# Five matmuls of a two-layer decoder trunk issued in two pieces each

## The chip, the cores and the metric

The kernel runs on one core of a Trainium2 chip. The metric is the device time of one execution in microseconds (us), the median of several runs.

## The reference

The input is x (256 tokens by 1024 features, float32) and a conditioning vector c. Two layers follow each other; each has a token mixer and then a gated feed-forward, and each of these four sub-layers is `x <- x + gate(c) * f(rmsnorm(x) * (1 + scale(c)) + shift(c))`:

```
mod = silu(c) @ w_ada[i] + b_ada[i]            # shift, scale, gate for mixer and feed-forward
layer 0 mixer: 8 heads of 128, causal attention inside one block of 256, QK RMS-norm
layer 1 mixer: b, c, u = split(h @ w_in);  y = (b * conv3(c * u)) @ w_out
feed-forward:  g, u = split(h @ w_gate_up);  y = (silu(g) * u) @ w_down      # width 2816
```

## The kernel before

All activations stay on the chip, features on the 128 partitions and the 256 tokens along the free dimension. Weights stream from HBM in tiles of 128 partitions by 8 x 256 float32 (1 MB), which SyncE's DMA queue loads into five `wf` buffers (`load`, L88). A float32 product is made of three products on TensorE: ScalarE rounds a weight tile to fp32r (`wh`, L98), VectorE takes the rest (`wl`, L99), both into three rotating buffers, and the activations are held in the same two parts. `mm3` (L246 to L250) issues the three matmuls of one 128x128 weight block by 256 token columns:

```
    def mm3(ps, lhs, rhs, first, last):
        (ah, al), (bh, bl) = lhs, rhs
        nc.tensor.matmul(ps, ah, bh, ...)   # L248
        nc.tensor.matmul(ps, ah, bl, ...)   # L249
        nc.tensor.matmul(ps, al, bh, ...)   # L250
```

The first operand is the stationary one; in the trace each matmul has a weight load of its own, even where the second matmul of a triple uses the same block as the first. `feat_gemm` runs over eight k (128 input features each) and two o (halves of 256 output features) and calls `mm3`: 48 matmuls for one weight tile.

The program in order: an opening with modulation sums and the first q/k products; attention and its output projection (`op_o`); the first feed-forward; the convolution; its output projection (`op_co`); the second feed-forward. A feed-forward (`ffn`, L426) has eleven steps j. Step 0 is `raw_gemm`: products of 258 columns (`raw_f`, `raw_m`) that run while the norm is still being made, ended by `settle`, two matmuls of one bf16 column (L396). Steps 1 to 10 are two `feat_gemm` each, gate (`pg`) and up (`pu`), 96 matmuls. Then `out_proj` makes `op_d`, 528 matmuls. The convolution has four steps with `pc`, `pu` and `pb`, of which step 0 takes `pc` and `pu` from `raw_gemm`.

VectorE also makes the modulation columns of the later sub-layers (`ada_piece`, `prod`, L109) between the weight tiles. A tile scheduler sets the order on each engine; weight tiles are asked for two ahead (`get`, AHEAD = 2). TensorE's instructions stand in program order.

Of the kernel before, what the change touches and what calls it, by code (L numbers as in the profile page):

```python
# [16 lines left out]
S = 256  # L17
D = 1024
KD = D // P
# [14 lines left out]
def trunk_kernel(ctx: ExitStack, tc: tile.TileContext, x_t, cols_in, scale_in, shift_in, ada_in, qk_rows, kv_in, o_in,  # L34
                 in_in, out_in, gu_in, down_in, out_f):
    nc = tc.nc
# [7 lines left out]
    def ps_gemm(name):  # L44
        return psum.tile([P, 2, CW], F32, tag="gemm", name=name, bufs=4)
# [104 lines left out]
    def new_pair(tag, name, nk):  # L150
        return tuple(pair_rows(room(tag + p, nk * S, name + p, F32R)) for p in "hl")
# [3 lines left out]
    hs = new_pair("h", "m0", KD)  # L155
# [11 lines left out]
    def conv_col(j, k):  # L167
        return v_cols[:, 32 + j * KD + k:][:, :1]
# [62 lines left out]
    def produce(upto):  # L231
        while pos[0] < len(chunks) and pos[0] <= upto:
            ch = chunks[pos[0]]
            if ch[0] == "a":
                ada_piece(*ch[1:])
            else:
                ready[ch[1]] = prep(ch[2], ch[3], "_".join(map(str, ch[1])), ch[1] in first_two)
            pos[0] += 1

    def get(key):  # L240
        n = place[key]
        produce(order[min(n + AHEAD, len(order) - 1)])
        return ready.pop(key)


    def mm3(ps, lhs, rhs, first, last):  # L246
        (ah, al), (bh, bl) = lhs, rhs
        nc.tensor.matmul(ps, ah, bh, start=first, stop=False, skip_group_check=True)  # L248
        nc.tensor.matmul(ps, ah, bl, start=False, stop=False, skip_group_check=True)  # L249
        nc.tensor.matmul(ps, al, bh, start=False, stop=last, skip_group_check=True)  # L250

    def feat_gemm(parts, xs, nk):
        xh, xl = xs
        for k in range(nk):
            for ps, (wh, wl) in parts:
                for o in range(2):
                    cs = slice(o * P, (o + 1) * P)
                    mm3(ps[:, o], (wh[:, k, cs], wl[:, k, cs]), (xh[:, k], xl[:, k]),
                        k == 0 and o == 0, k == nk - 1)

    def tok_gemm(parts, xs, nk, between={}):
        xh, xl = xs
        for k in range(nk):
            for fn, *args in between.get(k, ()):
                fn(*args)
            for ps, (wh, wl) in parts:
                for t in range(2):
                    ts = slice(t * P, (t + 1) * P)
                    mm3(ps[:, t], (xh[:, k, ts], xl[:, k, ts]), (wh[:, k], wl[:, k]),
                        k == 0 and t == 0, k == nk - 1)  # L270
# [117 lines left out]
    def split(dst, k, src, name, psum_src=False):  # L388
        nc.scalar.activation(dst[0][:, k], src, AF.Copy)
        nc.vector.tensor_sub(dst[1][:, k], src, dst[0][:, k].bitcast(F32))  # L390
# [7 lines left out]
    def raw_gemm(keys, norm, name):  # L398


        raw = norm.raw
        pss = [[psum.tile([P, S + 2], F32, tag=tag, name=f"raw_{name}_{i}{o}", bufs=n) for o in range(2)]
               for i, (tag, n) in enumerate((("gemm", 4), ("alt", 2)))]
        ws = [get(k) for k in keys]
        for k in range(KD):
            if k == 2:
                norm.rstd()
            if k == 4:
                rows = norm.rows()
                with tc.high_priority(400):  # L410
                    hs = modulated(norm.l, norm.sh, norm.scl, rows, name)
            for ps, (wh, wl) in zip(pss, ws):
                for o in range(2):
                    cs = slice(o * P, (o + 1) * P)
                    mm3(ps[o], (wh[:, k, cs], wl[:, k, cs]), (raw[0][:, k], raw[1][:, k]), k == 0, k == KD - 1)
        settle(name)
        res = []
        for i, tag in enumerate("sa"):
            y = tmp.tile([P, 2, S], F32, tag=tag, name=f"rawy_{name}_{i}")
            b = tmp.tile([P, 2], F32, tag="rawb", name=f"rawb_{name}_{i}")  # L420
            for o in range(2):
                nc.vector.tensor_copy(b[:, o:o + 1], pss[i][o][:, S:S + 1])
                nc.vector.tensor_mul(y[:, o], pss[i][o][:, :S], rows)
            res.append((y, b))
        return res[0], res[1], hs

    def ffn(l, norm, av, done):
        for j in range(KF // 2):
            if j == 0:
                (s, bs), (a, ba), hs = raw_gemm([("g", l, j), ("u", l, j)], norm, f"f{l}")  # L430
                for o in range(2):
                    nc.scalar.activation(s[:, o], s[:, o], AF.Silu, bias=bs[:, o:o + 1])
                    nc.vector.scalar_tensor_tensor(a[:, o], a[:, o], ba[:, o:o + 1], s[:, o], op0=ALU.add,
                                                   op1=ALU.mult)
            else:
                pg, pu = ps_gemm(f"pg_{l}_{j}"), ps_gemm(f"pu_{l}_{j}")
                feat_gemm([(pg, get(("g", l, j)))], hs, KD)
                feat_gemm([(pu, get(("u", l, j)))], hs, KD)
                s = tmp.tile([P, 2, S], F32, tag="s", name=f"s_{l}_{j}")
                nc.scalar.activation(s, pg, AF.Silu)  # L440
                a = tmp.tile([P, 2, S], F32, tag="a", name=f"a_{l}_{j}")
                nc.vector.tensor_mul(a, s, pu)
            split(av, slice(2 * j, 2 * j + 2), a, f"{l}_{j}")
        out_proj([[(("d", l, j, i), n) for i, n in enumerate((8, 8, 6))] for j in range(4)], av, l, G_F, done)
# [15 lines left out]
    def mod_columns(y, name):  # L460

        ps = ps_misc(f"mod_c_{name}")
        n = y.shape[1] // P
        for i in range(n):
            nc.tensor.matmul(ps[:, i:i + 1], y[:, i * P:(i + 1) * P], firsts, start=True, stop=True)
        return ps[:, :n]
# [71 lines left out]
    with tc.manual_schedule(engines={mybir.EngineType.PE, mybir.EngineType.DVE, mybir.EngineType.Activation}):  # L538
# [13 lines left out]
        for k in range(KD):  # L552
            nc.tensor.matmul(c_ps[k // 4][:, k % 4 * P:][:, :P], sc[:, k:k + 1].to_broadcast([P, P]), ident, start=True,
                             stop=True)
# [18 lines left out]
        ps = mod_columns(y, "sc0")  # L573
# [181 lines left out]
    zv, zraw = wide_pair("zv")  # L755
    n1 = Norm("n1", 1, SH_M, SC_M, zraw)
    ffn(0, n0, av, n1.take)


# [3 lines left out]
    for j in range(4):  # L763
        up = ups[j % 2]
        if j == 0:
            (cg, bc), (cu, bu), hs = raw_gemm([("cg", j), ("cu", j)], n1, "m1")
            for o in range(2):
                nc.scalar.activation(cg[:, o], cg[:, o], AF.Identity, bias=bc[:, o:o + 1])
                nc.vector.scalar_tensor_tensor(up[:, o, 2:], cu[:, o], bu[:, o:o + 1], cg[:, o], op0=ALU.add,
                                               op1=ALU.mult)  # L770
        else:
            pc, pu = ps_gemm(f"pc_{j}"), ps_gemm(f"pu_{j}")
            feat_gemm([(pc, get(("cg", j)))], hs, KD)
            feat_gemm([(pu, get(("cu", j)))], hs, KD)
            cg = tmp.tile([P, 2, S], F32, tag="s", name=f"cg_{j}")
            nc.scalar.activation(cg, pc, AF.Copy)
            with tc.high_priority(400):
                nc.vector.tensor_mul(up[:, :, 2:], cg, pu)
        pb = (ps_alt2 if j else ps_gemm)(f"pb_{j}")
        feat_gemm([(pb, get(("cb", j)))], hs, KD)  # L780
        y = tmp.tile([P, 2, S], F32, tag="a", name=f"y_{j}")
        with tc.high_priority(400):
            for o in range(2):
                k = 2 * j + o
                nc.scalar.activation(y[:, o], up[:, o, 0:S], AF.Copy, scale=conv_col(0, k))
            for i in (1, 2):
                for o in range(2):
                    nc.vector.scalar_tensor_tensor(y[:, o], up[:, o, i:i + S], conv_col(i, 2 * j + o), y[:, o],
                                                   op0=ALU.mult, op1=ALU.add)
        z = tmp.tile([P, 2, S], F32, tag="s", name=f"z_{j}")  # L790
        with tc.high_priority(400):
            nc.vector.tensor_mul(z, y, pb)
            split(zv, slice(2 * j, 2 * j + 2), z, f"z{j}")
# [6 lines left out]
    def store(k):  # L800
        if k >= KD - 2:
            nc.sync.dma_start(out_f[:, k], xT[:, k])
        elif k % 2:
            nc.sync.dma_start(out_f[:, k - 1:k + 1], xT[:, k - 1:k + 1])

    ffn(1, n2, av, store)


# [58 lines left out]
```

## Time and profile before

| what | value |
|---|---|
| runs | 597.25, 598.31, 599.61 us; median 598.31 |
| profiled execution | 597.81 us, span of its instructions 596.0 us |
| TensorE, weight loads | busy 587.8 and 579.0 us of the span |
| VectorE, ScalarE | busy 454.5 and 314.1 us |
| granted TensorE clock | 1.000 |
| DMA | 156 MB, 262 GB/s over the span |

The profile has one row for every matmul and one for every weight load (PEld). A row's start is measured; a matmul's end is modelled, and a row of 0.28 us overlaps the two that follow, so a busy TensorE can still be running at more than one pace. What shows the pace is the distance between starts.

### The profile page before, as it was taken

What the parts mean: (1) busy time and instruction counts of PE and PEld (TensorE: products, weight loads), DVE (VectorE), ACT (ScalarE), POOL (GpSimd) and SP (SyncE); (2) the same over time, 40 slices, a digit from 0 to 9 for tenths busy, and PEclk for the clock granted to TensorE, in tenths of its full rate; (3) what the DMA queues carried; (4) which work ended last, traced back from release to release, by engine and by line L of the source; (5) the groups of instructions that cost most, each with busy time, mean ns of one, the idle gap of its engine ahead of it and who ended that gap; (6) DMA issues with size and microseconds to landing.
All of it is one profiled execution on the core that took longest, in us unless ns stands there. A gap on an engine that the chain in (4) does not pass through costs nothing.

```text
span 596.0 us, 12024 instructions
## 1 busy us (share of the span) xinstructions
PE 587.8 (99%) x5036; PEld 579.0 (97%) x5036; DVE 454.5 (76%) x719; ACT 314.1 (53%) x526; POOL 1.1 (0%) x8
## 2 busy tenths in 40 slices
PE   7999999999999999999999999999999999999997
PEld 6899999999999999999999999999999999999997
DVE  4789898898988879877877998659987566564440
ACT  6457799596544544534444754437844554443330
POOL 0000000000000000000000000000000000000000
PEclk9999999999999999999999999999999999999999
DMA  8999988945897899777987477544486574655400
GB/s 323 392 373 411 361 332 300 369 162 180 329 388 296 303 358 356 268 279 276 330 317 292 148 293 278 207 142 184 170 323 249 206 283 164 252 186 190 165 19 18
DMA packets 25109, 156.04 MB, mean 262 GB/s; under 512 B 2784, under 2 KB 3168, under 8 KB 8928
## 3 DMA queue, kind: packets, MB, share of 16 engines
q1 hardware_dynamic: 25056, 155.28, 69.9%
q8 instruction: 39, 0.64, 0.4%
q14 instruction: 14, 0.11, 0.1%
HBM read 154.22 MB, written 1.05 MB: 261 GB/s over the span
## 4 chain that ended last, share of the span: by engine, by line
PE 89%; DVE 4%; DMA 3%; ACT 2%; issue 1%; SPq 0%; DVEq 0%; ACTq 0%
PE pu L250 7%; PE pu L249 7%; PE pu L248 7%; PE op_d L249 7%; PE op_d L248 7%; PE op_d L250 7%; PE pg L249 6%; PE pg L248 6%; PE pg L250 6%; PE op_o L248 1%; PE raw_f L248 1%; PE raw_f L249 1%; PE op_o L250 1%; PE op_co L250 1%; PE raw_f L250 1%; DMA wa<-in_ada_dram 1%
## 5 line engine op out<-in xcount | busy, mean ns | idle before, releaser
L109 DVE SCALAR_TENSOR_TENSOR prod<-wa,c_all 128x1024 f32<-128x1024 f32 x80 | 97.6, 1220 | 13.9 <-DMA wa<-in_ada_dram 13.0
L98 ACT ACTIVATE wh_d<-wf_d 128x1024 fp32r<-128x1024 f32 (+1 forms) x48 | 45.3, 981 | 67.2 <-issue 46.5
L99 DVE TENSOR_TENSOR wl_d<-wf_d,wh_d 128x1024 fp32r<-128x1024 f32 (+1 forms) x48 | 52.9, 1132 | 26.4 <-ACT wh_d L98 26.4
L98 ACT ACTIVATE wh_g<-wf_g 128x1024 fp32r<-128x1024 f32 x44 | 45.7, 1051 | 47.0 <-issue 47.0
L98 ACT ACTIVATE wh_u<-wf_u 128x1024 fp32r<-128x1024 f32 x44 | 44.5, 1051 | 48.4 <-issue 48.0
L99 DVE TENSOR_TENSOR wl_u<-wf_u,wh_u 128x1024 fp32r<-128x1024 f32 x44 | 52.2, 1219 | 16.7 <-ACT wh_u L98 16.5
L99 DVE TENSOR_TENSOR wl_g<-wf_g,wh_g 128x1024 fp32r<-128x1024 f32 x44 | 53.3, 1219 | 2.5 <-ACT wh_g L98 2.4
L249 PE MATMUL op_d<-a0l,wh_d 128*128 128x256 f32 x176 | 49.3, 280 | 0.0
L248 PE MATMUL op_d<-a0h,wh_d 128*128 128x256 f32 x176 | 49.1, 279 | 0.0
L250 PE MATMUL op_d<-a0h,wl_d 128*128 128x256 f32 x176 | 49.1, 279 | 0.0
L248 PE MATMUL op_d<-a1h,wh_d 128*128 128x256 f32 x176 | 48.6, 276 | 0.0
L249 PE MATMUL op_d<-a1l,wh_d 128*128 128x256 f32 x176 | 48.6, 276 | 0.0
L250 PE MATMUL op_d<-a1h,wl_d 128*128 128x256 f32 x176 | 48.6, 276 | 0.0
L249 PE MATMUL pg<-f0l,wh_g 128*128 128x256 f32 x160 | 44.8, 280 | 0.0
L249 PE MATMUL pu<-f0l,wh_u 128*128 128x256 f32 x160 | 44.8, 280 | 0.0
L248 PE MATMUL pg<-f0h,wh_g 128*128 128x256 f32 x160 | 44.7, 280 | 0.0
L250 PE MATMUL pg<-f0h,wl_g 128*128 128x256 f32 x160 | 44.6, 279 | 0.0
L248 PE MATMUL pu<-f0h,wh_u 128*128 128x256 f32 x160 | 44.6, 279 | 0.0
L250 PE MATMUL pu<-f0h,wl_u 128*128 128x256 f32 x160 | 44.6, 279 | 0.0
L248 PE MATMUL pg<-f1h,wh_g 128*128 128x256 f32 x160 | 44.2, 277 | 0.0
L249 PE MATMUL pg<-f1l,wh_g 128*128 128x256 f32 x160 | 44.2, 276 | 0.0
L250 PE MATMUL pg<-f1h,wl_g 128*128 128x256 f32 x160 | 44.2, 276 | 0.0
(296 smaller groups left out, 2024.8 us busy)
## 6 DMA issues: line engine op xcount, KB each, us to landing
wa<-in_ada_dram SPq DMA_DIRECT2D x40, 1024.0 KB, 5.3
wf_g<-in_gate_up_dram SPq DMA_DIRECT2D x22, 1024.0 KB, 4.9
wf_u<-in_gate_up_dram SPq DMA_DIRECT2D x22, 1024.0 KB, 4.9
wf_d<-in_down_dram SPq DMA_DIRECT2D x16, 1024.0 KB, 5.3
wf_d<-in_down_dram SPq DMA_DIRECT2D x8, 768.0 KB, 5.4
wa_sc<-in_scale_dram SPq DMA_DIRECT2D x8, 512.0 KB, 6.7
wa_sh<-in_shift_dram SPq DMA_DIRECT2D x8, 512.0 KB, 7.6
wf_qk<-in_qk_rows_dram SPq DMA_DIRECT2D x8, 512.0 KB, 6.5
```

The costliest lines, as they stand in the source:

```text
L98: nc.scalar.activation(wh[:, a:b], wf[:, a:b], AF.Copy)
L99: nc.vector.tensor_sub(wl[:, a:b], wf[:, a:b], wh[:, a:b].bitcast(F32))
L109: nc.vector.scalar_tensor_tensor(t, w, 1.0, c_all, op0=ALU.mult, op1=ALU.mult, accum_out=dst)
L248: nc.tensor.matmul(ps, ah, bh, start=first, stop=False, skip_group_check=True)
L249: nc.tensor.matmul(ps, ah, bl, start=False, stop=False, skip_group_check=True)
L250: nc.tensor.matmul(ps, al, bh, start=False, stop=last, skip_group_check=True)
```

## The change

`mm3` takes an argument `cut`. Where it is not zero, the third product is issued as two matmuls, one of the first `cut` columns and one of the rest, each with its own load of the same weight block. `feat_gemm` takes a list of cuts and spends one at each odd k with o = 1. The first feed-forward's `pg` of step 1 gets the cuts 128, 64, 192 and 96 (k = 1, 3, 5, 7); the convolution's `pc` of step 1 gets one cut of 128 (k = 1). Nothing else in the arithmetic changes, and the sums land in the same places.

```diff
-    def mm3(ps, lhs, rhs, first, last):
+    def mm3(ps, lhs, rhs, first, last, cut=0):
...
-        nc.tensor.matmul(ps, al, bh, start=False, stop=last, skip_group_check=True)
+        for a, b in ((0, cut), (cut, S)) if cut else ((0, None),):
+            nc.tensor.matmul(ps[:, a:b], al, bh[:, a:b], start=False, stop=last, skip_group_check=True)
 
-    def feat_gemm(parts, xs, nk):
+    def feat_gemm(parts, xs, nk, cuts=()):
+        cuts = list(cuts)
...
-                        k == 0 and o == 0, k == nk - 1)
+                        k == 0 and o == 0, k == nk - 1, cuts.pop(0) if o and k % 2 and cuts else 0)
...
-                feat_gemm([(pg, get(("g", l, j)))], hs, KD)
+                feat_gemm([(pg, get(("g", l, j)))], hs, KD, (128, 64, 192, 96) if (l, j) == (0, 1) else ())
...
-            feat_gemm([(pc, get(("cg", j)))], hs, KD)
+            feat_gemm([(pc, get(("cg", j)))], hs, KD, (128,) if j == 1 else ())
```

On TensorE, in the first feed-forward's step 1 (`pg_1`; `f0h`, `f0l` are the two parts of the activations, `wh_g_1`, `wl_g_1` those of the weights), the changed program has, from the first cut to the first matmul of `pu_1`:

```order
L248 MATMUL pg_1_1995<-f0h,wh_g_1_1816 128x256
L249 MATMUL pg_1_1995<-f0l,wh_g_1_1816 128x256
L252 MATMUL pg_1_1995<-f0h,wl_g_1_1817 128x128 x2
...
L252 MATMUL pg_1_1995<-f0h,wl_g_1_1817 128x64
L252 MATMUL pg_1_1995<-f0h,wl_g_1_1817 128x192
...
L252 MATMUL pg_1_1995<-f0h,wl_g_1_1817 128x96
L252 MATMUL pg_1_1995<-f0h,wl_g_1_1817 128x160
L248 MATMUL pu_1_1996<-f0h,wh_u_1_1824 128x256
```

Before, each pair was one row of 128x256 (at L250; the line is L252 now). The first pair is the twelfth matmul of `pg_1`, the others follow twelve matmuls apart; the third, of 192 and 64 columns, is left out above. With the one pair in the convolution's `pc_1` there are five, and no other row of TensorE moves up to the end of the program.

VectorE's rows are ordered a little differently, since the scheduler sees TensorE's added instructions. Behind the second half of `wl_u_2` stood before:

```order
L109 SCALAR_TENSOR_TENSOR prod_5_0_0_2119,mod<-wa_5_0_2117,c_all 128x1024
L442 TENSOR_TENSOR a_1_2111<-s_1_2109,pu_1_1996 128x512
L109 SCALAR_TENSOR_TENSOR prod_5_0_1_2121,mod<-wa_5_0_2117,c_all 128x1024
L99 TENSOR_TENSOR wl_g_3_2126<-wf_g_3_2123,wh_g_3_2125 128x1024
L390 TENSOR_TENSOR a0l<-a_1_2111,a0h 128x512
L99 TENSOR_TENSOR wl_g_3_2126<-wf_g_3_2123,wh_g_3_2125 128x1024
```

and stands now:

```order
L109 SCALAR_TENSOR_TENSOR prod_5_0_0_2123,mod<-wa_5_0_2121,c_all 128x1024
L109 SCALAR_TENSOR_TENSOR prod_5_0_1_2125,mod<-wa_5_0_2121,c_all 128x1024
L446 TENSOR_TENSOR a_1_2115<-s_1_2113,pu_1_1996 128x512
L99 TENSOR_TENSOR wl_g_3_2130<-wf_g_3_2127,wh_g_3_2129 128x1024 x2
L394 TENSOR_TENSOR a0l<-a_1_2115,a0h 128x512
```

One modulation sum (`prod`) and one half of `wl_g_3` stand ahead of work that they stood behind. Some twenty rows of VectorE and a few of ScalarE change places by one or two in this way, in the steps up to 5 of the first feed-forward and in the convolution. SyncE's order of DMAs is the same.

## Rows read from the trace of the kernel before

**Rows 1.** The profile page: the span, the busy time of the engines (with its share of the span and the instructions), and the shares of the chain that ended last.
```profile
span 596.0 us, 12024 instructions
...
PE 587.8 (99%) x5036; PEld 579.0 (97%) x5036; DVE 454.5 (76%) x719; ACT 314.1 (53%) x526; POOL 1.1 (0%) x8
...
PE 89%; DVE 4%; DMA 3%; ACT 2%; issue 1%; SPq 0%; DVEq 0%; ACTq 0%
```

**Rows 2.** Busy time by stretch: the first feed-forward behind its step 0, the convolution with its projection, the second feed-forward behind its step 0. Columns: the stretch, its length, busy us of each engine (x instructions), the granted clock, the DMA engines' mean busy share, GB/s.
```profile
143.60:318.40 174.80, 174.80 (x1486) 174.80 (x1485) 148.21 (x210) 81.15 (x104) 0.00 (x0) 1.00 0.82 306
331.20:411.00 79.80, 79.49 (x672) 79.09 (x672) 64.08 (x104) 44.38 (x67) 0.00 (x0) 1.00 0.55 203
424.00:590.00 166.00, 166.00 (x1466) 166.00 (x1466) 99.90 (x119) 73.15 (x88) 0.00 (x0) 1.00 0.52 189
```

**Rows 3.** The tile `op_d` of the first feed-forward, every third matmul (L249): duration in ns (least, median, most), first and last start in us.
```profile
L249 PE MATMUL op_d<-a0l,wh_d x176: 280/280/280, 256.4 to 318.2; 128*128 128x256 f32 x176
```

**Rows 4.** The same of the second feed-forward, from 547.4 us on.
```profile
L249 PE MATMUL op_d<-a1l,wh_d x133: 276/276/276, 547.4 to 592.3; 128*128 128x256 f32 x133
```

**Rows 5.** Timeline of matmuls and weight loads inside the two feed-forwards. Columns: start us, us, engine, line, operation, out<-in, size.
```profile
200.06 0.19 PEld L249 LDWEIGHTS pg<-f0l,wh_g 128*128 128x128 f32 x1
200.18 0.28 PE L249 MATMUL pg<-f0l,wh_g 128*128 128x256 f32 x1
...
500.02 0.19 PEld L249 LDWEIGHTS pg<-f1l,wh_g 128*128 128x128 f32 x1
500.13 0.28 PE L249 MATMUL pg<-f1l,wh_g 128*128 128x256 f32 x1
```

**Rows 6.** Timeline of TensorE in the opening, where the q products (weights stationary) are followed without a break by the k products (activations stationary).
```profile
27.43 0.28 PE L249 MATMUL pq<-m0l,wh_qk 128*128 128x256 f32 x1
...
28.02 0.28 PE L248 MATMUL pk<-wh_qk,m0h 128*128 128x256 f32 x1
...
28.37 0.28 PE L248 MATMUL pk<-wh_qk,m0h 128*128 128x256 f32 x1
...
28.71 0.28 PE L248 MATMUL pk<-wh_qk,m0h 128*128 128x256 f32 x1
```

**Rows 7.** Timeline of TensorE in the attention: four transposes of 128 columns inside the k products.
```profile
59.55 0.60 PE L654 MATMUL q_cols<-ident,q_y 128*128 128x128 f32 x4
59.90 0.37 PE L248 MATMUL pk<-wh_k,m0h 128*128 128x256 f32 x1
...
60.23 0.28 PE L250 MATMUL pk<-wh_k,m0l 128*128 128x256 f32 x1
...
60.68 0.28 PE L248 MATMUL pk<-wh_k,m0h 128*128 128x256 f32 x1
```

**Rows 8.** Timeline of TensorE in the projection `op_o`, around a short pause at 119 us.
```profile
118.62 0.28 PE L249 MATMUL op_o<-ovl,wh_o 128*128 128x256 f32 x1
...
118.86 0.28 PE L249 MATMUL op_o<-ovl,wh_o 128*128 128x256 f32 x1
...
119.13 0.38 PE L248 MATMUL op_o<-ovh,wh_o 128*128 128x256 f32 x1
119.35 0.28 PE L249 MATMUL op_o<-ovl,wh_o 128*128 128x256 f32 x1
...
119.69 0.28 PE L249 MATMUL op_o<-ovl,wh_o 128*128 128x256 f32 x1
```

**Rows 9.** The same, around a short pause at 127 us.
```profile
126.49 0.28 PE L250 MATMUL op_o<-ovh,wl_o 128*128 128x256 f32 x1
...
126.94 0.28 PE L248 MATMUL op_o<-ovh,wh_o 128*128 128x256 f32 x1
...
127.37 0.28 PE L248 MATMUL op_o<-ovh,wh_o 128*128 128x256 f32 x1
...
127.73 0.28 PE L248 MATMUL op_o<-ovh,wh_o 128*128 128x256 f32 x1
```

**Rows 10.** Timeline of TensorE at the first feed-forward's `settle`, the two matmuls of one column, and behind it.
```profile
143.02 0.20 PE L396 MATMUL settle_f<-one_b 128*128 128x1 bf16 x2
143.09 0.36 PE L248 MATMUL pg<-f0h,wh_g 128*128 128x256 f32 x1
143.29 0.28 PE L249 MATMUL pg<-f0l,wh_g 128*128 128x256 f32 x1
```

**Rows 11.** Timeline of TensorE in the convolution's step 1, at the third matmul of `pu`.
```profile
342.84 0.28 PE L249 MATMUL pu<-m1l,wh_cu 128*128 128x256 f32 x1
343.43 0.39 PE L250 MATMUL pu<-m1h,wl_cu 128*128 128x256 f32 x1 [0.31 <-DVE wl_cu L99]
343.66 0.28 PE L248 MATMUL pu<-m1h,wh_cu 128*128 128x256 f32 x1
...
344.01 0.28 PE L248 MATMUL pu<-m1h,wh_cu 128*128 128x256 f32 x1
```

**Rows 12.** Timeline of VectorE: the second half of `wl_cu` for that `pu`.
```profile
342.16 1.22 DVE L99 TENSOR_TENSOR wl_cu<-wf_cu,wh_cu 128x1024 fp32r<-128x1024 f32 x1
```

**Rows 13.** Timeline of VectorE and of TensorE: the second half of `wl_g` of the first feed-forward's step 2, and the matmul that first reads it.
```profile
150.15 1.22 DVE L99 TENSOR_TENSOR wl_g<-wf_g,wh_g 128x1024 fp32r<-128x1024 f32 x1
...
154.71 0.28 PE L250 MATMUL pg<-f0h,wl_g 128*128 128x256 f32 x1
```

## The prediction

> **What bounds the kernel now.** I read the page first: TensorE is busy 99% of the span, its weight loads 97%, and TensorE holds 89% of the chain that ended last [rows 1]. So the time is made on TensorE, and the question is what sets the distance between two matmuls there. I then took busy times by stretch. Three long stretches have the same kind of matmul (128x128 weights, 256 columns), all at granted clock 1.00, which is the 2.4 GHz level, and all with TensorE busy throughout. Yet the first feed-forward shows 1486 matmuls in 174.8 us, 117.6 ns each, the convolution 672 in 79.8 us, 118.8 ns with its pauses, and the second feed-forward 1466 in 166.0 us, 113.2 ns [rows 2].
>
> The tile view says the same without edges. In the first feed-forward's `op_d` every third matmul starts 61.8 us / 175 = 353.1 ns after the one before, 117.7 ns a matmul; in the second 44.9 us / 132 = 340.2 ns, 113.4 ns [rows 3, 4]. The durations are constant to the nanosecond (280 and 276 ns), so these are two steady paces, not a mean of fast and slow pieces. I call them the slow and the fast pace; they differ by 4.4 ns, 3.8%.
>
> Where the 4.4 ns sit is seen beside the loads. The load for a matmul starts with the matmul before it, and the matmul starts 0.12 us after its load began in the slow stretch, 0.11 us in the fast one [rows 5]. So each matmul waits for its own weights, and the chain load, matmul, next load is a little longer at the slow pace. VectorE is not the reason: the same program text in the second feed-forward is only better supplied (VectorE 60% busy there, 85% in the first), but both paces also stand within `op_o`, a few microseconds apart with the same tiles [rows 8, 9].
>
> What changes the pace is the last thing to read. In the opening the q products run at (28.02 − 27.43)/5 = 118 ns; where operands change places and k products follow, without any idle time, the pace is (28.71 − 28.37)/3 = 113 ns [rows 6]. In `op_o` a pause of some 0.15 us turned 120 ns into 113 ns, and another turned 113 ns back into 120 ns [rows 8, 9]. Four transposes of 128 columns left fast products fast: (60.68 − 60.23)/4 = 113 ns [rows 7]. So a pace holds until something uneven comes, and is then settled anew. In the first feed-forward nothing uneven comes for the 1484 matmuls behind its start.
>
> **The change part by part.**
>
> *The first feed-forward's four cuts.* Each replaces one matmul by two, with one more weight load. No row has a 256-column product cut in two, so I bound the price of the extra matmul. From below: the two one-column matmuls of `settle` pass in 0.07 us together, 0.035 us each [rows 10]. From above: a start behind a pause is followed by the next only 0.23 us later [rows 11]. The nearest rows are the matmuls that wait for their own load, 0.11 us [rows 5], since the piece has a full 128x128 load too; the transposes of 128 columns take 0.35/4 = 0.09 us each to the next start [rows 7]. I take 0.113 us: four cost 0.45 us (ends 0.14 and 0.92).
>
> *What the cuts do to the pace.* This is the large term. I read the rows so: the load and the columns of the matmul before it run side by side [rows 5], and at the slow pace they hold each other up by 4.4 ns each time. A piece of 64 to 192 columns ends its stream early, so the load behind it should not be held up, and the chain starts again from another place. I expect that one of four unlike pieces brings the fast pace, and that the fast pace, where the load alone sets the time, is not lost to a shorter stream (the transposes did not end it [rows 7]). Behind the first cut stand 10 × 96 − 12 + 528 = 1476 matmuls, up to the end of `op_d`: 1476 × 4.4 ns = 6.5 us. If only the fourth cut does it, 36 fewer, 0.16 us less. At the worst the term is nothing, or the pace stays slow.
>
> Two pages speak against this term. The Trainium skill, in "TensorE: Matmul & The Clock Gate", section "Wait — 56ns, not 53.3ns?", gives back-to-back matmuls one distance for a column count, columns ÷ 2.4 GHz plus about 2.5 ns; that is an estimate of 109 ns at 256 columns, and the cuts would add some 0.01 us and save nothing. This trace has two distances for one shape, both longer, so here the measurement decides. The same page, section "Step-by-step: what each phase is for", says that loading the next weights takes no read bandwidth from the running matmul; by that the length of a piece could not matter, which is the first rival below.
>
> *VectorE, ScalarE and the queues.* The supply must now come 3.8% sooner. VectorE is busy 148.2 of 174.8 us [rows 2]; the fast stretch would have 168.3 us, so 88%, and DMA goes from 0.82 to 0.85. The tightest weights are those of step 2: their second half is ready at 151.4 us and first read at 154.7 us [rows 13], 3.3 us of cover against 0.43 us a step. The scheduler's swap puts one modulation sum in front of a half weight tile, 1.2 us of the cover. I take nothing; were the cover gone, the first wait would be at `pg_3`, some 1 us.
>
> *The convolution's cut.* It stands in `pc_1`, ahead of a wait that no cut removes: the third matmul of `pu_1` waits for VectorE's second half of `wl_cu`, which ends at 343.4 us, and starts 0.59 us behind its forerunner instead of 0.12 [rows 11, 12]. The extra 0.113 us lies in those 0.47 us, and so does whatever 36 faster matmuls would gain (0.16 us). Behind the wait the pace is settled anew; before, it came out slow, (344.01 − 343.66)/3 = 117 ns [rows 11]. I take the slow pace again: 0 us.
>
> *The sum.* −6.5 + 0.45 = −6.0 us. The profiled execution took 597.81 us, 1.8 us around its span; it becomes 591.8. The median of the runs lies 0.5 us higher, so I forecast 592.3 us.
>
> **The rivals.**
>
> *The pace stays slow.* The cuts cost their slots and nothing else: 598.3 + 0.45 = 598.8 us. For it: four pairs are few, and `settle`, also a short disturbance, left the first feed-forward slow. Against it: the paces did change at lesser events [rows 6].
>
> *The convolution goes fast too.* Behind its wait stand 46 + 48 + 288 + 192 = 574 matmuls; × 4.4 ns = 2.5 us, 589.8 us. The wait's new start decides, and it moves by tenths of a microsecond with what stands before.
>
> *The second feed-forward falls to the slow pace.* It is fast today behind the same `settle` that left the first slow. Its pace is decided at about 424 us, behind products of 258 columns; what comes in there is changed only if the convolution or its wait is. Price 1488 × 4.4 = 6.5 us. With the gain in the first it ends at 592.3 + 6.5 = 598.8, no change; without that gain at 598.8 + 6.5 = **605.3 us, slower**. Its sign is the pace of `pg` just behind 424 us.
>
> *Supply too late.* The first feed-forward goes fast but waits for weights: 592.3 plus 1 to 3 us.
>
> That the change does not do what it says I rule out: TensorE's order has the five pairs and nothing else.
>
> **How the numbers follow.** A measurement of this kernel can tell 0.5%, 3.0 us, from no change. Chances: first feed-forward fast alone 0.30 (592.3); convolution too 0.26 (589.8); pace stays slow 0.22 (598.8); gain in the first and loss in the second feed-forward 0.12 (about 598.8, or 596.3 with the convolution); loss alone 0.07 (605.3); late supply 0.03. Faster is the first two and half of the last: 0.58. Slower is the loss alone and an unforeseen wait: 0.08. The rest, 0.34, is within 0.5%. The forecast's own range is 591.2 to 593.4 us, the scatter of the runs. The range for 8 in 10 must reach from the convolution's case, 589.8 less 1.0 for scatter, to the slow pace with its dearer cuts (598.3 + 0.92, rounded up): 588.8 to 599.4 us. It leaves the loss alone outside.
>
> **What would show it.** Right: `op_d` of the first feed-forward at 340 ns for three, the change of pace within the 48 matmuls of `pg_1`, the stretch from there to the end of `op_d` near 168 us, the wait at `pu_1` still there, and 353 ns for three behind it. The extra slots are wrong if the second piece of a pair starts more than 0.2 us behind the first. The whole is wrong if `op_d` still shows 353 ns, or if the second feed-forward's does.

## The result and the profile after

The changed kernel takes 593.15 us (median of ten executions, 591.13 to 597.28); ten executions of the kernel before, taken beside it, have 597.29 us (595.08 to 599.61). The ratio is 0.9943, with a 95% interval of 0.9924 to 0.9962, so the change gains time: 4.1 us, where I forecast 6.0. The ten times fall into two groups: six at 591.1 to 593.5 us and four at 595.8 to 597.3 us. The profiled execution is the slowest of the ten, 597.28 us, which is useful: it shows the gain and, later, the loss of nearly all of it. The rows for [rows 1] are now these.

```profile
span 595.5 us, 12032 instructions
...
PE 584.4 (98%) x5041; PEld 575.9 (97%) x5041; DVE 454.1 (76%) x719; ACT 315.2 (53%) x526; POOL 1.1 (0%) x8
...
PE 85%; DMA 7%; DVE 5%; ACT 2%; issue 1%; DVEq 0%; ACTq 0%; SPq 0%
```

The span is 0.5 us shorter than before, TensorE is busy 3.4 us less, and DMA's share of the chain that ended last has risen from 3% to 7%. So something of the gain went to waiting for data. The tile `op_d` of the first and of the second feed-forward, every third matmul (duration in ns; first and last start in us), against [rows 3, 4]:

```profile
L249 PE MATMUL op_d<-a0l,wh_d x176: 276/276/276, 253.6 to 313.1; 128*128 128x256 f32 x176
...
L249 PE MATMUL op_d<-a1l,wh_d x133: 276/276/276, 546.8 to 591.7; 128*128 128x256 f32 x133
```

In the first, three matmuls now take 59.5/175 = 340 ns instead of 353; the second is unchanged. The change of pace stands at the fourth cut. Timeline of TensorE around the first, third and fourth cut (start us, us, engine, line, operation, tiles, size; a pair of pieces is one row, x2):

```profile
145.29 0.34 PE L252 MATMUL pg<-f0h,wl_g 128*128 128x128 f32 x2
145.47 0.34 PE L248 MATMUL pg<-f0h,wh_g 128*128 128x256 f32 x1
...
148.34 0.30 PE L252 MATMUL pg<-f0h,wl_g 128*128 128x192 f32 x2
148.48 0.36 PE L248 MATMUL pg<-f0h,wh_g 128*128 128x256 f32 x1
148.68 0.28 PE L249 MATMUL pg<-f0l,wh_g 128*128 128x256 f32 x1
...
149.50 0.28 PE L252 MATMUL pg<-f0h,wl_g 128*128 128x256 f32 x1
...
149.86 0.35 PE L252 MATMUL pg<-f0h,wl_g 128*128 128x96 f32 x2
150.04 0.32 PE L248 MATMUL pu<-f0h,wh_u 128*128 128x256 f32 x1
150.19 0.28 PE L249 MATMUL pu<-f0l,wh_u 128*128 128x256 f32 x1
...
150.53 0.28 PE L249 MATMUL pu<-f0l,wh_u 128*128 128x256 f32 x1
```

From the third cut to the fourth the pace is still slow, (149.50 − 148.68)/7 = 117 ns; behind the fourth it is (150.53 − 150.19)/3 = 113 ns, and so it stays up to the end of `op_d`. Where the time then went, by stretch (columns as in [rows 2]): the fast stretch, the convolution's opening in two pieces, the convolution, the second feed-forward.

```profile
150.20:313.20 163.00, 163.00 (x1441) 163.00 (x1440) 137.41 (x192) 76.16 (x96) 0.00 (x0) 1.00 0.87 320
313.30:321.90 8.60, 5.44 (x43) 4.94 (x42) 7.89 (x12) 3.90 (x7) 0.00 (x0) 1.00 0.78 288
321.90:325.40 3.50, 3.50 (x19) 3.50 (x19) 2.01 (x3) 1.06 (x2) 0.00 (x0) 0.52 0.97 353
...
331.30:411.00 79.70, 79.70 (x681) 79.70 (x680) 63.00 (x99) 43.25 (x65) 0.00 (x0) 1.00 0.54 198
424.00:590.00 166.00, 166.00 (x1467) 166.00 (x1466) 99.40 (x117) 72.58 (x86) 0.00 (x0) 1.00 0.52 189
```

TensorE idles 3.2 us in the first 8.6 us of the opening. Then its granted clock falls from 1.00 to the 1.2 GHz level for some 3 us (0.52 over the third stretch). The waits of TensorE from 143 to 424 us (who waits, for whom; us in total, times, longest) name the idle time:

```profile
PE raw_m L252 <- DVE wl_cu L99: 2.0, 1, 2.0
PE ms_n L346 <- ACT sq_n L318: 0.8, 1, 0.8
PE ms_n L345 <- DVE ss_n L326: 0.3, 1, 0.3
```

Before, no such wait stood there. Starts taken from the timelines split the program at its marks: the two `settle` of the feed-forwards, `settle_m` of the convolution and the last `op_d` matmul of each feed-forward. In us, for the kernel before, after, and three runs of the next section:

| stretch | before | after | e0_again | e5_early_sums | e9_conv_step2 |
|---|---|---|---|---|---|
| first feed-forward, `settle_f` to last `op_d` | 175.3 | 169.3 | 169.3 | 169.3 | 172.2 |
| convolution's opening, to `settle_m` | 12.7 | 18.1 | 12.8 | 13.3 | 12.7 |
| convolution and `op_co`, to `settle_f` | 92.7 | 91.9 | 93.2 | 91.9 | 90.8 |
| second feed-forward, to last `op_d` | 168.7 | 168.7 | 168.7 | 168.7 | 168.7 |

The first feed-forward gains 6.0 us. In this execution the convolution's opening then gives back 5.4 of them.

### The profile page after: what moved, and what is told of

Same layout as the page of the kernel before. It is cut to its first block, busy times and chain, and to the rows that moved or that the text cites. A ratio compares the mean times of both kernels' runs of the same rounds, so it can differ in the third digit from the quotient of the medians.

```text
span 595.5 us, 12032 instructions
## 1 busy us (share of the span) xinstructions
PE 584.4 (98%) x5041; PEld 575.9 (97%) x5041; DVE 454.1 (76%) x719; ACT 315.2 (53%) x526; POOL 1.1 (0%) x8
## 4 chain that ended last, share of the span: by engine, by line
PE 85%; DMA 7%; DVE 5%; ACT 2%; issue 1%; DVEq 0%; ACTq 0%; SPq 0%
PE pu L248 7%; PE pu L252 7%; PE pu L249 7%; PE pg L248 6%; PE pg L252 6%; PE pg L249 6%; DMA wa<-in_ada_dram 5%; PE op_d L249 4%; PE op_d L252 4%; PE op_d L248 4%; DVE prod L109 1%; PE op_o L248 1%; PE raw_f L248 1%; PE pb L248 1%; PE raw_f L249 1%; PE raw_f L252 1%
## 5 line engine op out<-in xcount | busy, mean ns | idle before, releaser
L99 DVE TENSOR_TENSOR wl_u<-wf_u,wh_u 128x1024 fp32r<-128x1024 f32 x44 | 52.3, 1220 | 13.3 <-ACT wh_u L98 13.1
L249 PE MATMUL op_d<-a0l,wh_d 128*128 128x256 f32 x176 | 48.6, 276 | 0.0
L252 PE MATMUL op_d<-a0h,wl_d 128*128 128x256 f32 x176 | 48.6, 276 | 0.0
L249 PE MATMUL op_d<-a1l,wh_d 128*128 128x256 f32 x176 | 48.6, 276 | 0.0
L252 PE MATMUL op_d<-a1h,wl_d 128*128 128x256 f32 x176 | 48.6, 276 | 0.0
L252 PE MATMUL pg<-f0h,wl_g 128*128 128x256 f32 (+3 forms) x164 | 44.4, 275 | 0.0
L249 PE MATMUL pg<-f0l,wh_g 128*128 128x256 f32 x160 | 44.2, 276 | 0.0
L249 PE MATMUL pu<-f0l,wh_u 128*128 128x256 f32 x160 | 44.2, 276 | 0.0
L252 PE MATMUL pu<-f0h,wl_u 128*128 128x256 f32 x160 | 44.2, 276 | 0.0
L249 PE MATMUL pg<-f1l,wh_g 128*128 128x256 f32 x160 | 44.2, 276 | 0.0
L252 PE MATMUL pg<-f1h,wl_g 128*128 128x256 f32 x160 | 44.2, 276 | 0.0
```

The source lines that it names most:

```text
L99: nc.vector.tensor_sub(wl[:, a:b], wf[:, a:b], wh[:, a:b].bitcast(F32))
L252: nc.tensor.matmul(ps[:, a:b], al, bh[:, a:b], start=False, stop=last, skip_group_check=True)
```

## The wait that took the gain back

What is late is read on VectorE. Its timeline at the convolution's opening, before:

```profile
311.50 1.23 DVE L109 SCALAR_TENSOR_TENSOR prod<-wa,c_all 128x1024 f32<-128x1024 f32 x1 [2.17 <-DMA wa<-in_ada_dram]
...
316.07 2.36 DVE L99 TENSOR_TENSOR wl_cu<-wf_cu,wh_cu 128x1024 fp32r<-128x1024 f32 x2
```

and after:

```profile
310.57 1.23 DVE L109 SCALAR_TENSOR_TENSOR prod<-wa,c_all 128x1024 f32<-128x1024 f32 x1 [2.56 <-DMA wa<-in_ada_dram]
...
315.13 2.36 DVE L99 TENSOR_TENSOR wl_cu<-wf_cu,wh_cu 128x1024 fp32r<-128x1024 f32 x2
317.41 0.48 DVE L362 SCALAR_TENSOR_TENSOR xT<-op_d,mod,xT 128x256 f32<-128x256 f32 x1
```

The first matmul that reads `wl_cu` on TensorE, before:

```profile
319.37 0.28 PE L250 MATMUL raw_m<-zvh,wl_cu 128*128 128x258 f32 x1
```

and after, with the start of the 1.2 GHz stretch:

```profile
314.11 0.28 PE L249 MATMUL raw_m<-zvl,wh_cu 128*128 128x258 f32 x1
316.41 0.39 PE L252 MATMUL raw_m<-zvh,wl_cu 128*128 128x258 f32 x1 [2.02 <-DVE wl_cu L99]
...
318.91 0.38 PE L345 MATMUL ms_n<-inv_d,ss_n 128*128 128x1 f32 x2 [0.33 <-DVE ss_n L326]
320.10 0.38 PE L346 MATMUL ms_n<-inv_d,sq_n 128*128 128x1 f32 x2 [0.81 <-ACT sq_n L318]
...
322.33 0.42 PE L252 MATMUL raw_m<-zvh,wl_cu 128*128 128x258 f32 x1
322.55 0.42 PE L248 MATMUL raw_m<-zvh,wh_cg 128*128 128x258 f32 x1
```

Before, the first half of `wl_cu` was ready at 316.07 + 2.36/2 = 317.25 us and first read at 319.37: 2.1 us of cover. TensorE now arrives 5.1 us sooner (start of the last `op_d` matmul, 318.3 to 313.2), VectorE only 0.9 us sooner (316.07 to 315.13), because a `prod` ahead waits for its modulation weights `wa` from DMA. 2.1 + 0.9 − 5.1 = −2.1 us, and the wait is 2.0. It does not end there: the residual `xT` of `op_d` stands behind `wl_cu` on VectorE, so the norm's sums are late too and `ms_n` waits twice. After these pauses some fifteen matmuls run 0.21 us apart instead of 0.12, another 1.4 us. The wait, the norm's 1.1 us and the clock's 1.4 us are 4.5 of the 5.4 us; the rest is not assigned.

## The experiments

The kernel before was run again with each set: 597.38, 597.51, 597.33 and 597.46 us (medians of 11 to 17). "Sums" below are the eight modulation pieces (`ada`) that are loaded in the down-projection's part of the DMA stream.

**e0_again: the changed kernel unaltered**, in three rounds. No edit.

> The changed kernel once more, unaltered. Theory (the gain on TensorE is partly given back at the convolution's opening, where VectorE's wl_cu and the modulation sums come from a DMA stream that is no faster than before): the first feed-forward's op_d is again at 340 ns for three, there is again a wait before the convolution's products at about 314 us, of 0 to 3 us, and the time lies between 591 and 597.5 us according to that wait. Rival (the pace itself is drawn anew in each execution): op_d is at 353 ns in some profile of the same program, and the slower executions are those.

Measured: nine of ten executions took 591.8 to 599.8 us, median 596.2; the tenth took 3318.85 us, which nothing on record explains. The ratio of the nine is 0.9966 (0.9934 to 0.9998), a gain barely clear of none. Over both sets of the changed kernel, 19 executions, the median is 594.9 us, so the 4.1 us of the first ten are on the lucky side: nine executions lie at 593.5 us or below and ten at 594.9 or above. The shorter nine have a mean granted clock of 0.999 or 1.000; eight of the longer ten have 0.996 or 0.997, as the profiled execution above with its 3 us at the lower level has (0.997). The longer times thus mostly go with a fall of the clock. The profiled execution of e0_again took 593.29 us. It has the same fast stretch (169.3 us) and no wait at the opening (12.8 us), because VectorE was earlier:

```profile
306.84 1.22 DVE L109 SCALAR_TENSOR_TENSOR prod<-wa,c_all 128x1024 f32<-128x1024 f32 x1 [2.18 <-DMA wa<-in_ada_dram]
...
311.40 2.35 DVE L99 TENSOR_TENSOR wl_cu<-wf_cu,wh_cu 128x1024 fp32r<-128x1024 f32 x2
```

The same program thus has its first half of `wl_cu` at 312.6 us in one execution and at 316.3 in another. The pace is in both; the cover is in one. In e0_again the wait at `pu_1` of [rows 11] is there (0.2 us).

**e1_first_cut: the 128 cut alone**, and **e2_last_cut: the 96 cut alone**; neither has a cut in the convolution.

```diff
-(128, 64, 192, 96) if (l, j) == (0, 1)
+(128,) if (l, j) == (0, 1)             # e1
+(0, 0, 0, 96) if (l, j) == (0, 1)      # e2
```

> Only the first cut (128) in the first feed-forward, none in the convolution. Theory (a cut settles the pace anew, and the first one came out slow): the spacing stays at 117.8 ns through op_d (353 ns for three), time 597 to 598. Rival (any cut frees the load chain, and the first would have been enough with time): 113.3 ns, time near 592.

> Only the fourth cut (96 and 160 columns at k = 7), none in the convolution. Theory (it is the place and size of this one cut that settles the fast pace): 113.3 ns behind it and op_d at 340 ns for three, time 591.5 to 597. Rival (the shifts of all four add up, and the last alone is not enough): 117.8 ns through op_d, time 597 to 598.

Measured: 597.29 and 597.19 us. The tile `op_d`, e1 and then e2:

```profile
L249 PE MATMUL op_d<-a0l,wh_d x176: 279/279/279, 256.6 to 318.5; 128*128 128x256 f32 x176
...
L249 PE MATMUL op_d<-a0l,wh_d x176: 280/280/280, 256.6 to 318.4; 128*128 128x256 f32 x176
```

It is slow in both (61.9/175 and 61.8/175, some 353 ns for three). The 96 cut brings the fast pace only when others stand ahead of it, so my theory that the piece itself decides missed.

**e3_second_ff: the four cuts in the second feed-forward**, which is fast without them, and nowhere else.

```diff
-(128, 64, 192, 96) if (l, j) == (0, 1)
+(128, 64, 192, 96) if (l, j) == (1, 1)
```

> The four cuts stand in the second feed-forward's pg of step 1, which is at the fast pace before, and nowhere else. Theory (at the fast pace the load alone sets the time, so a shorter stream cannot end it): the second op_d stays at 340 ns for three and the time is that of the kernel before plus 0.3 us. Rival (a cut draws the pace anew whatever it was): 353 ns for three behind the cuts, 6.5 us more than before, about 604 us.

Measured: 605.65 us, so slower by 8.3. In the stretches of the table above, 6.9 of it lie in the second feed-forward (175.6 against 168.7) and 0.8 in the convolution, where the waits differ. The cuts 128 and 64 left the pace fast; at 192 it fell, and 96 did not bring it back. Timeline of TensorE and, behind it, the tile `op_d` of the second feed-forward:

```profile
428.21 0.28 PE L249 MATMUL pg<-f1l,wh_g 128*128 128x256 f32 x1
...
428.89 0.28 PE L249 MATMUL pg<-f1l,wh_g 128*128 128x256 f32 x1
429.00 0.30 PE L252 MATMUL pg<-f1h,wl_g 128*128 128x192 f32 x2
...
429.35 0.28 PE L249 MATMUL pg<-f1l,wh_g 128*128 128x256 f32 x1
...
430.06 0.28 PE L249 MATMUL pg<-f1l,wh_g 128*128 128x256 f32 x1
```

```profile
L249 PE MATMUL op_d<-a1l,wh_d x171: 280/280/280, 540.1 to 600.1; 128*128 128x256 f32 x171
```

Six matmuls take 0.68 us ahead of the cut and 0.71 behind it; in `op_d` three take 60.0/170 = 353 ns. A fast pace can be lost to a shorter stream.

**What the two paces are.** Averaged over hundreds of starts, the slow 353 ns are not three equal distances. One of the three products is followed by 118.33 ns, the other two by 117.3 to 117.7, and which one it is differs by stretch: the first product in the first feed-forward before (476 distances from 150 to 318.4 us), the third in e1_first_cut behind its cut (476, from 150 to 318 us), the second in the convolution before (190, from 344 us to the end of `op_co`). I call these the slow phases A, C and B; F is the fast pace. A cut takes one to another (an empty place was not seen):

| phase ahead | 128 | 64 | 192 | 96 |
|---|---|---|---|---|
| A | C | A | C | A |
| C | C | C | B | C |
| B | F | | | F |
| F | F | F | A | F |

The change's list walks A, C, C, B, F: only the 192 cut leads from C to B, and only from B does a cut lead to F. So the fourth cut brings the fast pace here because the three before it end at B. By the table 128, 192 and 96 should do it without the 64.

**e4_three_cuts: without the 64 cut.**

```diff
-(128, 64, 192, 96) if (l, j) == (0, 1)
+(128, 0, 192, 96) if (l, j) == (0, 1)
```

> The second cut (64) is left out, the others (128, 192, 96) stay at their places in the first feed-forward; no cut in the convolution. Theory (the slow pace has three phases, told by the product behind which the long distance of 118.33 ns stands: A behind the first, B behind the second, C behind the third; in the traces so far 128 leads from A to C, 64 from C to C, 192 from C to B, 96 from B to the fast pace): A, C, C, B, fast; op_d at 340 ns for three, as with all four. Rival (four chances, drawn anew each time, one of which came out): no reason for the same end; 353 ns for three as likely as not.

Measured: fast behind the 96 cut, as the walk says, with `op_d` at 59.5/175 = 340 ns for three:

```profile
L249 PE MATMUL op_d<-a0l,wh_d x176: 276/276/276, 252.8 to 312.3; 128*128 128x256 f32 x176
```

The time is 595.61 us, since this execution waited at the opening again (1.0 us for `wl_cu`, 1.1 for the norm).

**e10_forty: forty cuts**, four in each step of the first feed-forward, in a fixed unordered list, to fill the table.

```diff
-(128, 64, 192, 96) if (l, j) == (0, 1)
+FORTY[4 * j - 4:4 * j] if l == 0
```

> Forty cuts, four in each pg of the first feed-forward's steps 1 to 10, of 64, 96, 128 or 192 columns in a fixed mixed order; no cut in the convolution, modulation pieces as in the changed kernel. Theory: the pace behind a cut depends only on the phase ahead of it and on its size, so a pair of phase and size that comes again leads to the same phase again, and the pairs seen before (A 128 to C, C 64 to C, C 192 to B, B 96 to fast, A 96 to A, fast 128 and fast 64 to fast, fast 192 to A) all hold. Rival (each cut draws by chance): repeated pairs disagree. Time 592 to 602, by how many steps end fast, with 40 slots of 0.113 us, 4.5 us, in it.

Measured: 607.67 us, above what I expected: it waited 2.2 us at the opening and 1.6 in two waits of `op_d`. The first of the two (at 260 us) left the fast pace as it was, the second ended it at 277 us. The phases came out as the theory says: wherever a phase and a size occur again, here and in the other runs, the outcome is the same (C and 96 twelve times, A and 96 six times). The table holds these outcomes.

**e5_early_sums: the cuts as in the change, and the sums earlier.** The last two sums stood near the end of the down-projection's stream, in front of the convolution's weights; now one piece stands behind each of the first eight tiles. **e6_early_alone** has this and no cuts.

```diff
-    mix(ada(1, G_M) + ada(1, SC_F), dn)
+    adas = ada(1, G_M) + ada(1, SC_F)
+    for i, ch in enumerate(dn):
+        chunks.append(ch)
+        chunks.extend(adas[i:i + 1])
```

> The changed kernel with the eight modulation pieces that stand between the down-projection's weight tiles asked for one behind each of the first eight tiles, instead of spread to the last. Theory (part of the gain is given back at the convolution's opening because the modulation pieces and wl_cg, wl_cu come late from the DMA stream): TensorE's wait at about 314 us goes, the slower executions near 596.5 go with it, median 591 to 592.5, ratio to the kernel before 0.988 to 0.992. Rival (the wait is bound by the stream's bytes, wherever the pieces stand): the same two groups of times, median 593 to 596.5.

> The kernel before (no cuts) with the earlier modulation pieces alone. Theory (at the slow pace the stream is just in time, so an earlier one gives nothing): 597 to 598, the same as before. Rival (the earlier pieces are a gain of their own): 594 to 596.

Measured: e5 591.70 us (591.26 to 592.40), ratio 0.9898 (0.9881 to 0.9915); e6 597.32, ratio 0.9995 (0.9977 to 1.0013). By itself the new order is worth nothing; with the cuts the gain is 5.8 us instead of 4.1, and none of the five executions falls into the second group of times. Five are few: e8 and e9 below are the same program up to the end of `op_d`, and some of their executions are slow again, by a wait at another place. `wl_cu` comes early on VectorE:

```profile
309.64 2.36 DVE L99 TENSOR_TENSOR wl_cu<-wf_cu,wh_cu 128x1024 fp32r<-128x1024 f32 x2 [0.34 <-ACT wh_cu L98]
```

That is 310.8 us for the first half, where TensorE starts its last `op_d` matmul at 312.4.

**e11_sums_at_two: the eight pieces behind the third to the tenth tile**, with the convolution's cuts of e9 below.

```diff
-        chunks.extend(adas[i:i + 1])
+        chunks.extend(adas[i - 2:i - 1] if i > 1 else ())
```

> The four cuts in the first feed-forward, the cuts 128, 192, 96 in the convolution's step 2, and the eight modulation pieces behind the third to tenth tile of the down-projection, so that neither its first four tiles nor the convolution's first two stand behind a crowd of them. Theory (a wait of some tenths of a microsecond for wl_d at about 268 us threw the fast pace away in the slower executions of the two kernels before this one, and a wait at the convolution's opening in the changed kernel): neither wait is there, 589.3 to 590.3 in every execution, ratio 0.987. Rival (the stream is short of bytes at the fast pace wherever the pieces stand): a wait at another place, and again two groups of times, 590 and 592 to 596.

Measured: 594.86 us (591.06 to 598.81), ratio 0.9961 (0.9938 to 0.9984). This missed: the scatter is back, and the profiled execution waits 1.0 us for `wl_cu` once more, as the rival says (a wait at another place). The down-projection has twelve tiles. With two of them free ahead of the convolution's weights the wait at the opening came back; with four, as in e5 and e7 to e9, no profiled execution has it.

**e7_early_conv96, e8_conv_step1, e9_conv_step2: the convolution**, all with the sums of e5. e7 has (128, 0, 192, 96) in the feed-forward and one cut of 96 in `pc_2`; e8 and e9 keep the four cuts there and put 128, 192, 96 into `pc_1` or `pc_2`.

```diff
-feat_gemm([(pc, get(("cg", j)))], hs, KD, (128,) if j == 1 else ())
+feat_gemm([(pc, get(("cg", j)))], hs, KD, (96,) if j == 2 else ())            # e7
+feat_gemm([(pc, get(("cg", j)))], hs, KD, (128, 192, 96) if j == 1 else ())   # e8
+feat_gemm([(pc, get(("cg", j)))], hs, KD, (128, 192, 96) if j == 2 else ())   # e9
```

> Earlier modulation pieces, cuts 128, 192, 96 in the first feed-forward, and in the convolution one cut of 96 in step 2 (in place of 128 in step 1). Theory of phases: behind the convolution's wait at pu_1 the phase was B (long distance behind the second product) in the traces with a wait, and 96 leads from B to the fast pace; then op_co runs at 340 ns for three and 1.7 us more are gained, median 589.5 to 591. If the phase there is A, 96 leaves it at A: 353 ns for three, time as with the earlier pieces alone. Rival (a cut draws a pace by chance): either, without regard to the phase ahead of it.

> The kernel with earlier modulation pieces (591.7 us, ratio 0.990); the convolution's step 1 gets three cuts, 128, 192 and 96 at k = 1, 3, 5, in place of one of 128. Theory of phases: A to C to B to the fast pace, inside pc_1. If no wait follows at pu_1, op_co runs at 340 ns for three and the time falls by 2.2 us to 589.5; if the faster pc_1 brings the wait for wl_cu back, the pace behind it is settled anew and slow, and the time stays at 591.5 to 592.5. Rival (cuts act by chance): neither tied to that wait.

> The same three cuts in the convolution's step 2 instead, behind the place of the wait, and none in step 1. Theory of phases: the phase ahead is A in the earlier-pieces kernels without a wait there (long distance behind the first product), so C, B and the fast pace follow; 449 matmuls at 4.4 ns less the three slots are 1.6 us, 590.0. If a wait has left phase B ahead, what 128 does from B has not been seen, and op_co may stay at 353 ns. Rival (chance): 353 ns whatever the phase ahead.

Measured: e7 593.81 us, ratio 0.9928 (0.9904 to 0.9951): the phase ahead of its cut was A, and 96 left it at A. Its time is 2.1 us above that of e5, where I expected none, for the reason at the end of this section. e8 590.57 us, 0.9875 (0.9844 to 0.9906), and e9 589.95 us, 0.9881 (0.9852 to 0.9909): both walked A, C, B, F. The projection `op_co` of e9 is fast, 22.0/63 = 349 ns with its pauses; in the kernel before it was 22.2/63 = 352. First e9, then before:

```profile
L252 PE MATMUL op_co<-zvl,wh_co x64: 276/276/279, 384.0 to 406.0; 128*128 128x256 f32 x64
...
L249 PE MATMUL op_co<-zvl,wh_co x64: 279/279/280, 388.7 to 410.9; 128*128 128x256 f32 x64
```

These two have the lowest medians here. The 412 matmuls that e9's cuts make fast are worth 412 × 4.4 ns = 1.8 us, less some 0.3 for the cuts. In the table of stretches its convolution is 1.1 us shorter than that of e5 (90.8 against 91.9), since a pause of 0.4 us in `op_co` takes another part. The medians of e9 and e5 differ by 1.75 us, but they stand beside different sets of the kernel before, and the intervals of their ratios overlap, so the times alone don't show the gain. The profiled execution of e9, at 592.96 us, is one of its two slowest and shows another way to lose the pace, a short wait in `op_d` of the first feed-forward:

```profile
267.79 0.28 PE L252 MATMUL op_d<-a0l,wh_d 128*128 128x256 f32 x1
268.90 0.39 PE L255 MATMUL op_d<-a0h,wl_d 128*128 128x256 f32 x1 [0.83 <-DVE wl_d L99]
```

Behind it 394 matmuls are slow: 1.7 us, and with the wait's own 1.0 that is nearly all of the 2.9 us by which its first feed-forward exceeds that of e5 in the table of stretches. The profiled execution of e8 has this wait too, and in e7 one of 0.2 us there did the same to 393 matmuls. Ahead of this `wl_d` VectorE has three sums, where the changed kernel has one; in e5 the same three come 3.4 us sooner and there is no wait. So the new order seems to take the wait from the opening and to put a smaller one here in some executions; no run tests that by itself.

## Why the prediction held, and where it did not

**The pace.** Right in place and size: slow to fast inside `pg_1`, `op_d` at 340 ns for three, the fast stretch ended by nothing up to `op_d`'s end. The first feed-forward is shorter by 6.0 us in two profiled executions (169.3 in both, against 175.3), and the terms −6.5 + 0.45 gave −6.05.

**The time.** Partly luck. 593.15 us is 0.85 above the forecast of 592.3, but the kernel before was 1.0 us faster beside it than the 598.31 I started from, which hides half of the 1.9 us by which the gain fell short. In e0_again the same program has a median of 596.2 us: inside the range for 8 in 10, outside the forecast's own range.

**The slots.** Right. The second piece starts 59, 30, 90 and 43 ns behind the first (cuts 128, 64, 192, 96), and from the first piece to the second full matmul behind the pair it takes 347, 343, 340 and 338 ns, where two slow distances take 235. The four cost 0.43 us together.

**The convolution's cut.** Right that it gains nothing: A became C, both slow. Wrong about the wait at `pu_1`, which I took to be there in any case and listed as a sign of being right. The profiled executions of before, e0_again, e3 and e10 have it; those of after, e1, e2, e4 to e9 and e11 do not. Where it is absent it can't hide the cut's slot, about 0.1 us. What decides it is not shown.

**The second feed-forward.** Right: it stayed fast. That its pace can be lost at 6.5 us or more, the price of the slower rival, was shown by e3_second_ff (6.9 us).

**The supply: the step that was mis-sized.** I wrote that the tightest weights are those of step 2, with 3.3 us of cover [rows 13], and took 0. The stretch of the first feed-forward did stay without a wait. But a stage that ends 5.1 us sooner asks sooner for the next stage's weights, and those had 2.1 us of cover at 319.37 us, in a row that I had not read. The rival "supply too late" named late weights, but inside the first feed-forward, at 1 to 3 us and a chance of 0.03. The wait came one stage later and cost up to 5.4 us with the norm and the clock behind it, in some executions only: ten of the 19 are in the longer group of times. Over the first ten 1.9 us of the median are missing (6.0 less 4.1); with the sums earlier, 0.2 (6.0 less 5.8).

**The reason for the pace.** Wrong. I held that a piece ends its stream early and so frees the load behind it, that one of four unlike pieces would do so, and that a shorter stream does not end the fast pace. By that reason one cut should be enough; e1 and e2 have one each and stay slow. e3 refutes the last part: a cut of 192 ended the fast pace. What decides is the phase ahead together with the width, and that the four widths happened to walk from A to F was luck. The Trainium skill, in "TensorE: Matmul & The Clock Gate", section "Step-by-step: what each phase is for", says that loading the next weights takes no read bandwidth from the running matmul; going by that alone, the length of a piece would not matter. Here it does: from C a cut of 192 leads to B, and 64, 96 and 128 do not. What makes the slow pace 13 ns longer in three matmuls is not shown here.

**Left open.** Why the DMA stream is earlier in some executions of the same program. From 150 to 331 us VectorE waited for `wa` 11.7 us before, 22.4 after, 15.3 in e0_again and 16.2 in e5. The largest goes with the wait at the opening, but what made those loads late is not shown.

## What to carry to other kernels

On an engine that is busy throughout, read the distance between starts: a steady state can have several paces, and a small irregularity can move it from one to another, in either direction. Here it did so the same way each time, given the phase ahead and the width. When a stage is made shorter, look up the cover of the first weights of the next stage, not only of its own, and subtract the whole gain from it. A pause there costs more than its length, since it can take the pace or the clock with it.

## What was not expected of the hardware

- One shape (128x128 weights, 256 columns, each with its load) has two steady paces at the same granted clock of 1.00, 113.3 and 117.8 ns, and the slower has three phases. Cuts move between them in a fixed way, by the phase ahead and the width of the first piece.
- A wait of 0.2 us ended a fast stretch for the next 393 matmuls (1.7 us, e7), while one of over a microsecond left the fast pace as it was (e10, at 260 us).
- The granted clock fell to the 1.2 GHz level for some 3 us at 322 us, after a stretch of 8.6 us in which TensorE was idle for 3.2 us in several pauses; the matmuls then stood 0.21 us apart. The profiled executions of e4 and e11, with waits of 1.0, 0.8 and 0.3 us at the same place, show it too; that of e10, with 2.2, 0.8 and 0.3 us, does not.
- A piece of 64 columns let the second piece start 30 ns behind it, a piece of 192 columns 90 ns, each with a load of its own.
